# One DMA ring instead of two, with 64 KiB runs per partition, in a split-SiLU-multiply kernel

## The chip, the cores and the metric

The kernel runs on one core of a Trainium2 chip. The metric is device time in microseconds (us), the median of several runs. The core is fed by 16 DMA engines. A *ring* is the queue of transfers that one issuing engine owns: SP's ring is q1 in the profile and ACT's ring is q10. Both are worked off by the same 16 DMA engines.

## The reference

```python
batch, seq, dim = (32, 512, 2048)                # x: float32
half_dim = x.shape[-1] // 2
x1, x2 = x[..., :half_dim], x[..., half_dim:]
silu_x1 = x1 * (1 / (1 + np.exp(-x1)))
return (silu_x1 * x2).astype(np.float32)         # (32, 512, 1024)
```

That is 16384 rows of 8 KiB in and 4 KiB out: 134.2 MB to load and 67.1 MB to store, with one SiLU and one multiply per output element.

## The kernel before

The 128 rows per partition are cut into tiles of 4, then twenty times 6, then 4 rows. A load is 48 KiB per partition and a store 24 KiB. Loads are issued by SP and stores by ACT.

```python
K_MAIN, K_EDGE, KC = 6, 4, 2
in_pool  = ctx.enter_context(tc.tile_pool(name="in_pool", bufs=2))
out_pool = ctx.enter_context(tc.tile_pool(name="out_pool", bufs=4))
# ... plan = [(row0, K)]: 4, 6 x 20, 4 rows per partition ...
for bi, (row0, K) in enumerate(plan):
    xv = x_flat[row0:row0 + P * K].rearrange("(p k) d -> p k d", k=K)
    ov = out_flat[row0:row0 + P * K].rearrange("(p k) d -> p k d", k=K)
    xt = in_pool.tile([P, KT, in_cols], dt, name="xt")
    nc.sync.dma_start(out=xt[:, :K, :], in_=xv)                      # SP's ring
    ot = out_pool.tile([P, KT, half], dt, name="ot")
    for c in range(0, K, KC):
        ce = min(c + KC, K)
        nc.scalar.activation(out=ot[:, c:ce, :], in_=xt[:, c:ce, :half],
                             func=mybir.ActivationFunctionType.Silu)
        nc.vector.tensor_mul(out=ot[:, c:ce, :], in0=ot[:, c:ce, :],
                             in1=xt[:, c:ce, half:])
    nc.scalar.dma_start(out=ov, in_=ot[:, :K, :])                    # ACT's ring
```

## Time and profile before

| what | value | view |
|---|---|---|
| time | 474.58 us (474.44 to 474.65, 3 runs) | timed runs |
| span of the profiled run | 473.1 us | page, head |
| DMA engines' time in packets | 65.9% + 33.0% | page, part 3 |
| DVE, ACT busy | 30%, 25% | page, part 1 |

From the page of the kernel before: busy time per engine (part 1), DMA busy in tenths and GB/s in 40 slices of the span (part 2), the two rings with packets, MB and share of 16 engines (part 3), and the chain that ended last (part 4).

```profile
DVE 142.9 (30%) x64; ACT 118.9 (25%) x65; POOL 0.2 (0%) x4
...
DMA  8999999999999999999999999999999999999995
GB/s 355 449 398 424 432 430 455 420 428 451 414 432 441 432 443 432 416 434 447 426 428 457 418 435 436 443 432 424 432 443 418 438 453 411 451 432 418 433 420 244
...
q1 hardware_dynamic: 3168, 134.22, 65.9%
q10 hardware_dynamic: 3168, 67.11, 33.0%
...
DMA 78%; DVE 14%; ACT 4%; issue 1%; DVEq 0%; SPq 0%; ACTq 0%
```

The DMA engines are busy for nine tenths or more of every slice but the first and the last, and no compute engine is busy a third of the time. The kernel is bound by the DMA engines. What can be gained is the idle time at the ends and the time that packets take beyond their bytes. The last slice, at 244 GB/s, shows the end. The busy time by stretches of the kernel before, near its end (columns: stretch and its length; busy us of DVE, ACT and POOL; TensorE clock; DMA share; GB/s):

```profile
455.00:460.00 5.00, 0.00 (x0) 0.71 (x1) 0.00 (x0) 1.00 0.94 405
460.00:465.00 5.00, 3.77 (x2) 3.00 (x2) 0.00 (x0) 1.00 0.58 251
465.00:470.00 5.00, 0.72 (x1) 0.00 (x0) 0.00 (x0) 1.00 0.74 315
470.00:475.00 5.00, 0.00 (x0) 0.00 (x0) 0.00 (x0) 1.00 0.25 105
```

And its instructions in order of time (start us, duration, engine, line, operation):

```profile
459.29 3.71 ACT L64 ACTIVATE ot<-xt 128x2048 f32<-128x2048 f32 x2 [10.47 <-DMA xt<-in_x_dram]
461.23 4.49 DVE L69 TENSOR_TENSOR ot<-ot,xt 128x2048 f32<-128x2048 f32 x2 [9.29 <-ACT ot L64]
465.76 0.34 ACTq L74 DMA_DIRECT2D out_dram<-ot  x1
```

The last load lands at 459.3 us, but the last store is issued only at 465.8 us. In between the engines drain what is queued and then stand idle (share 0.58 between 460 and 465 us).

Part 3 of the page is made from records of single DMA packets: start, duration, size, ring. One packet here is the run of one partition. A record does not name its DMA engine, but engines can be told apart, since a packet starts within a few ns of the end of the one before it on the same engine. All that is said below of packets was worked out from these records in that way. In the kernel before, 48 KiB packets take 1815 ns, 24 KiB packets 912 ns, 32 KiB 1211 to 1213 ns and 16 KiB 611 ns. This is a straight line: 27.2 GB/s per engine plus about 8 ns per packet. I call the time on this line *nominal*, and what a packet takes beyond it *stretch*.

### The profile page before, as it was taken

The page shows a single profiled execution, that of the slowest core. Times are in us where ns is not written, and L with a number is a line of the kernel's source. Part 1 is how long each engine was busy: PE and PEld are TensorE (multiplying, and loading weights), DVE is VectorE, ACT ScalarE, POOL GpSimd, SP SyncE. Part 2 cuts the span into 40 slices and gives each one's busy share as a digit, 9 for nine tenths or more (in the row PEclk, how much of TensorE's full clock was granted, in tenths as well). Part 3 has the DMA queues.
Part 4 walks back from the last instruction along what each step waited for, and adds up shares of the span by engine and source line. Part 5 has one row for each costly group of instructions (what it writes and reads, how often), then busy time and mean ns, then how long its engine had stood idle before and what let it go on. Part 6 is the DMA issues. An engine that isn't in the chain of part 4 may idle for free.

```text
span 473.1 us, 296 instructions
## 1 busy us (share of the span) xinstructions
DVE 142.9 (30%) x64; ACT 118.9 (25%) x65; POOL 0.2 (0%) x4
## 2 busy tenths in 40 slices
DVE  0323505050514324050505142231505050513323
ACT  1340404041231404040413214040404042231411
POOL 0000000000000000000000000000000000000000
DMA  8999999999999999999999999999999999999995
GB/s 355 449 398 424 432 430 455 420 428 451 414 432 441 432 443 432 416 434 447 426 428 457 418 435 436 443 432 424 432 443 418 438 453 411 451 432 418 433 420 244
DMA packets 6338, 201.35 MB, mean 426 GB/s; under 512 B 704, under 2 KB 704, under 8 KB 704
## 3 DMA queue, kind: packets, MB, share of 16 engines
q1 hardware_dynamic: 3168, 134.22, 65.9%
q10 hardware_dynamic: 3168, 67.11, 33.0%
q14 instruction: 2, 0.02, 0.0%
HBM read 134.22 MB, written 67.11 MB: 426 GB/s over the span
## 4 chain that ended last, share of the span: by engine, by line
DMA 78%; DVE 14%; ACT 4%; issue 1%; DVEq 0%; SPq 0%; ACTq 0%
DMA xt<-in_x_dram 78%; DVE ot L69 14%; ACT ot L64 4%; DVEq L100 0%; SPq L59 0%; ACTq L64 0%
## 5 line engine op out<-in xcount | busy, mean ns | idle before, releaser
L69 DVE TENSOR_TENSOR ot<-ot,xt 128x2048 f32<-128x2048 f32 x64 | 142.9, 2287 | 322.8 <-ACT ot L64 322.8
L64 ACT ACTIVATE ot<-xt 128x2048 f32<-128x2048 f32 x64 | 117.6, 1899 | 343.4 <-DMA xt<-in_x_dram 343.4
L64 ACT ACT_TABLE_LOAD x1 | 1.3, 1283 | 0.7 <-PEq L89 0.7
L89 POOL MEMSET const-bfloat16-1.0<- 128x1 bf16 x1 | 0.1, 103 | 0.0
L89 POOL MEMSET const-uint8-127<- 128x1 uint8 x1 | 0.1, 103 | 0.0
L89 POOL MEMSET const-float32-1.0<- 128x1 f32 x1 | 0.1, 100 | 0.0
L89 POOL MEMSET const-float32-0.0<- 128x1 f32 x1 | 0.1, 99 | 0.2 <-issue 0.2
## 6 DMA issues: line engine op xcount, KB each, us to landing
xt<-in_x_dram SPq DMA_DIRECT2D x20, 6144.0 KB, 34.8
out_dram<-ot ACTq DMA_DIRECT2D x20, 3072.0 KB, 27.8
xt<-in_x_dram SPq DMA_DIRECT2D x2, 4096.0 KB, 20.7
out_dram<-ot ACTq DMA_DIRECT2D x2, 2048.0 KB, 15.4
```

The source lines that it names most:

```text
L64: nc.scalar.activation(out=ot[:, c:ce, :], in_=xt[:, c:ce, :half], func=mybir.ActivationFunctionType.Silu,)
L69: nc.vector.tensor_mul(out=ot[:, c:ce, :], in0=ot[:, c:ce, :], in1=xt[:, c:ce, half:],)
L89: nc = _bacc.Bacc("TRN2", target_bir_lowering=False, num_devices=1)
```

## The change

The intent: fewer, larger runs; one ring, so that every transfer has the engines to itself; and an end in which stores are queued ahead of the last multiply. Tiles become 8 rows, so a load is 64 KiB per partition. Two tiles share one output buffer, stored in one run of 64 KiB per partition. Everything is issued by SP in the order L0 L1 L2 S01 L3 L4 S23 L5 ... (L is a load, S a store of two tiles). The last two tiles are stored in a half and four quarters.

```diff
-    K_MAIN = 6
-    K_EDGE = 4
+    K = 8
-    out_pool = ctx.enter_context(tc.tile_pool(name="out_pool", bufs=4))
+    out_pool = ctx.enter_context(tc.tile_pool(name="out_pool", bufs=1))
+    xv = x_flat.rearrange("(n p h k) d -> n h p k d", p=P, h=2, k=K)
+    ov = out_flat.rearrange("(n p k) d -> n p k d", p=P, k=2 * K)
...
+    def load(i):
+        xt = in_pool.tile([P, K, in_cols], dt, name="xt")
+        nc.sync.dma_start(out=xt, in_=xv[i // 2, i % 2])
+        loaded[i] = xt
+    load(0)
+    load(1)
+    for i in range(n_tiles):
+        xt = loaded.pop(i)
+        if i % 2 == 0:
+            ot = out_pool.tile([P, 2 * K, half], dt, name="ot")
+        o0 = (i % 2) * K
         for c in range(0, K, KC):
+            o = slice(o0 + c, o0 + c + KC)
             ...                                  # SiLU and multiply as before, on ot[:, o, :]
+            if i == n_tiles - 1:
+                nc.sync.dma_start(out=ov[i // 2][:, o, :], in_=ot[:, o, :])
-        nc.scalar.dma_start(out=ov, in_=ot[:, :K, :])
+        if i == n_tiles - 2:
+            nc.sync.dma_start(out=ov[i // 2][:, :K, :], in_=ot[:, :K, :])
+        elif i % 2 == 1 and i < n_tiles - 2:
+            nc.sync.dma_start(out=ov[i // 2], in_=ot)
+        if i + 2 < n_tiles:
+            load(i + 2)
```

More of the change, by code (lines that the diff above doesn't have):

```diff
@@ L24 @@
     dt = x_flat.dtype
-    K_MAIN = 6
-    K_EDGE = 4
+    K = 8
     KC = 2
+    n_tiles = num_rows // (P * K)
+    assert n_tiles * P * K == num_rows
     in_pool = ctx.enter_context(tc.tile_pool(name="in_pool", bufs=2))
-    out_pool = ctx.enter_context(tc.tile_pool(name="out_pool", bufs=4))
-    rows_per_part_total = num_rows // P
-    rem = rows_per_part_total - 2 * K_EDGE
-    if rem > 0 and rem % K_MAIN == 0:
-        plan_k = [K_EDGE] + [K_MAIN] * (rem // K_MAIN) + [K_EDGE]
-    else:
-        plan_k = []
-        rem = rows_per_part_total
-        while rem > 0:
-            k = min(K_MAIN, rem)
-            plan_k.append(k)
-            rem -= k
-    plan = []
-    row = 0
-    for k in plan_k:
-        plan.append((row, k))
-        row += P * k
-    assert row == num_rows
-    KT = max(K_MAIN, K_EDGE)
-    for bi, (row0, K) in enumerate(plan):
-        xv = x_flat[row0:row0 + P * K].rearrange("(p k) d -> p k d", k=K)
-        ov = out_flat[row0:row0 + P * K].rearrange("(p k) d -> p k d", k=K)
-        xt = in_pool.tile([P, KT, in_cols], dt, name="xt")
-        nc.sync.dma_start(out=xt[:, :K, :], in_=xv)
-        ot = out_pool.tile([P, KT, half], dt, name="ot")
+    out_pool = ctx.enter_context(tc.tile_pool(name="out_pool", bufs=1))
+    xv = x_flat.rearrange("(n p h k) d -> n h p k d", p=P, h=2, k=K)
+    ov = out_flat.rearrange("(n p k) d -> n p k d", p=P, k=2 * K)
+    loaded = {}
+    def load(i):
[4 more added lines that the diff above has]
+    load(1)
+    ot = None
+    for i in range(n_tiles):
[3 more added lines that the diff above has]
+        o0 = (i % 2) * K
         for c in range(0, K, KC):
-            ce = min(c + KC, K)
+            o = slice(o0 + c, o0 + c + KC)
             nc.scalar.activation(
-                out=ot[:, c:ce, :],
-                in_=xt[:, c:ce, :half],
+                out=ot[:, o, :],
+                in_=xt[:, c:c + KC, :half],
                 func=mybir.ActivationFunctionType.Silu,
@@ L69 @@
             nc.vector.tensor_mul(
-                out=ot[:, c:ce, :],
-                in0=ot[:, c:ce, :],
-                in1=xt[:, c:ce, half:],
-            )
-        nc.scalar.dma_start(out=ov, in_=ot[:, :K, :])
+                out=ot[:, o, :],
+                in0=ot[:, o, :],
+                in1=xt[:, c:c + KC, half:],
+            )
+            if i == n_tiles - 1:
[6 more added lines that the diff above has]
+            load(i + 2)
 _INS = ['x']
```

## The prediction

> **What bounds the kernel now.** The 16 DMA engines. The page's part 1 shows DVE busy 30%, ACT 25%; part 2 DMA at 9 tenths in every slice but the first and last; part 3 65.9% + 33.0% of 16 engines' span; the chain of waits is 78% loads. The packet records behind part 3: a 48 KiB load packet takes 1815 ns, a 24 KiB store packet 912 ns, the edge tiles' 32 and 16 KiB ones 1211 and 611 ns. That is a line of 36.8 ns per 1000 bytes (27.2 GB/s per engine, 435 GB/s in all) plus about 8 ns per packet; the 435 agrees with the ceiling in the Trainium skill, "DMA: Bandwidth & Descriptors", Specifications. The rate is the same with loads alone (12 to 19 us), stores alone (the last 5 us) and both, and between two loads on one ring the gap is a few ns. So neither a second ring nor mixing costs anything visible.
>
> Sum for before: 1.7 us to the first packet + 466.7 us of packets per engine + 3.3 us idle per engine in the last 12 us + about 1.5 us closing = 473.1 us of span; timed, 1.5 us more.
>
> **What the change does.**
> - Packets: loads and full stores become 64 KiB (estimate from the line: 2419 ns). 224 packets per engine for 352, at 8 ns: -1 us; fewer semaphore packets: -0.1 us.
> - One ring, with SP waiting in order: L2, S01, L3, L4, S23, ... The output buffer is single, so a pair's first SiLU waits for the preceding store. With 1.9 + 4 x 2.29 = 11 us of compute per tile and an estimated 19.5 us per 8 MB transfer, the next load is issued about 13 us after that store lands, while another load still runs. The ring never runs dry; margin about 6 us. No gain, no loss.
> - Tail: when the last load lands, 4 MB of store (9.7 us) is queued, and four 1 MB stores follow from about 6 us on, 2.3 us apart, each lasting 2.4 us. So the idle 3.3 us at the end go: the main gain.
> - Head: unchanged; loads 0 and 1 are both queued.
> - A transient in before (36 load packets between 21 and 28 us took 2.0 to 2.6 us, about 1 us per engine) may or may not return.
>
> Sum for after: 1.7 + 464.9 + 0.6 (slow first packets) + 0.2 + 1.5 = 469 us of span, 470.4 us timed: 0.9% faster. All of it is on the critical path, since DMA is.
>
> Predicted 470.4 us, range 468.5 to 475. Faster by over 2%: 0.03 (it needs engines above 27.2 GB/s); within 2%: 0.89; slower by over 2%: 0.08.
>
> **What would show it.** 64 KiB packets at about 2419 ns, loads and stores alike; DMA at 9 tenths until the last slice; SiLU waiting for the store once per pair, without a hole in DMA; no idle in the last 12 us.
>
> **What would make it wrong.** (a) Address stride: a partition's loads now stand 128 KiB apart, so engines work at multiples of 512 KiB; the same page, "Latency and other measured facts", has copies losing rate at power-of-two pitches from 512 KiB up (207 of 214 GB/s). Packets above 2.42 us would show it; no run here does yet. (b) 64 KiB packets cut in two (+1 us). (c) A bubble where load and store switch on one ring, hidden before by the other ring. (d) The margin eaten by engines out of step: a hole per pair.

## The result, and the profile after

The changed kernel took 474.33 us (473.35 to 474.90, 4 runs) beside 474.55 us for the kernel before in the same rounds. The ratio is 0.9991, with a 95% interval of 0.9977 to 1.0006: no difference clear of noise. All outputs are right. I had predicted 470.4 us. The time lies inside my range, but the gain that I forecast, 4 us, is not there.

The same lines of the page of the changed kernel (parts 1 to 4):

```profile
DVE 142.4 (30%) x64; ACT 118.2 (25%) x65; POOL 0.2 (0%) x4
...
DMA  8999989999999999999999999999999999999996
GB/s 355 443 443 443 443 355 443 443 443 443 438 427 405 416 443 443 443 443 438 393 438 427 432 443 438 443 443 427 421 421 432 427 445 443 443 427 421 410 420 279
...
q1 hardware_dynamic: 4032, 201.33, 98.9%
...
DMA 79%; DVE 15%; ACT 3%; SPq 1%; DVEq 0%; issue 0%
```

The engines are as busy as before, now on one ring, and they moved the same bytes with 36% fewer packets. Yet the share of their time is still 98.9%. So the packets took longer than their bytes. Slice 5 (counted from 0, 59 to 71 us) drops to 355 GB/s. It is the slice in which the first store begins, and later slices dip to 405 and 393. A slice is a coarse measure, though, with packets of 2.4 us in slices of 11.8 us; the packet records are sharper.

Waits of the compute engines of the changed kernel (us in total, times, longest), then its stretches near the end, to be laid beside those of before:

```profile
ACT ot L58 <- DMA out_dram<-ot: 225.2, 7, 33.2
ACT ot L58 <- DMA xt<-in_x_dram: 115.7, 9, 20.5
```

```profile
455.00:460.00 5.00, 5.00 (x3) 4.81 (x3) 0.00 (x0) 1.00 0.87 374
460.00:465.00 5.00, 3.34 (x2) 0.00 (x0) 0.00 (x0) 1.00 1.01 428
465.00:470.00 5.00, 0.00 (x0) 0.00 (x0) 0.00 (x0) 1.00 0.77 324
470.00:475.00 5.00, 0.00 (x0) 0.00 (x0) 0.00 (x0) 1.00 0.02 8
```

The SiLU waits for the store seven times, once per pair after the first, as predicted, and this opens no hole in DMA. The hole between 460 and 465 us is filled (1.01 for 0.58). But look at the last row: in the last 3 us of the span the DMA share over 5 us is 0.02, and not 0. One engine is still at work. The packet records say it plainly: fifteen engines end between 468.1 and 469.6 us, and the sixteenth at 471.7 us, alone for its last seven packets.

The account, per engine, for both kernels and for a second profile of the changed one (run e0 below):

| term, us | predicted for after | before | after | after, second profile |
|---|---|---|---|---|
| packets at nominal time | 464.9 | 465.9 | 464.8 | 464.8 |
| stretch of each engine's first packet | 0.6 | 0.7 | 0.6 | 0.7 |
| stretch at the first store | left open, 0 in the sum | 1.1 | 1.2 | 1.1 |
| stretch later on | 0 | 0.1 | 1.4 | 1.6 |
| idle for want of transfers, at the end | 0 | 3.3 | 0 | 0 |
| last engine behind the mean of the 16 | 0.2 | 0.1 | 2.6 | 2.4 |

The rest of the span is the time to the first packet (1.7 us; 1.9 us in the mean of the engines), the closing (1.3 to 1.4 us), and overlaps of successive records (3 to 4 ns each; 1.4 us per engine before, 0.9 us after), which my sum left out. Nominal time came out as predicted: over 9 in 10 of the 64 KiB packets take 2415 to 2421 ns, loads and stores alike. The 3.3 us of idle at the end went, as predicted. They came back as 1.3 to 1.5 us more stretch and as one engine 2.4 to 2.6 us behind the mean. Both profiles of the changed kernel are of runs slower than the median (474.79 us for 474.33, 474.64 us for 474.43), and its runs scatter over 1.6 and 2.0 us, those of the kernel before in the same rounds over 0.2 and 0.9 us. So the stretch and the lag of a typical run may be somewhat smaller.

Where does the stretch stand? In the changed kernel, nearly all packets over 2480 ns are an engine's *last load packet before a store*: near 58, 117, 175, 233, 292, 350, 409 and 447 us. Those are the ends of L2, L4, L6 and so on, after which the ring holds a store. The change from store to load shows nothing, nor does the one from load to load. Over loads and stores that follow without such a change, the spread of the engines stays as it is, to 0.2 us. At each change from load to store the distance grows. Here is how far the last engine ends a transfer behind the first, at loads that stand just before a store in the changed kernel (two profiles), and at similar times in run e2, which has two rings:

```text
about us    22   61   119  177  235  293  351  410  448
after       0.5  0.6  0.8  1.3  1.7  2.1  2.7  3.2  3.5
after (e0)  0.8  0.8  0.9  1.3  2.0  2.4  2.8  3.1  3.5
e2          0.6  0.5  0.5  0.5  0.5  0.5  1.2  1.4  1.4
```

The kernel before, with two rings, behaves like e2: its first store leaves the engines 2.0 us apart, and at 433 us they are still 2.0 us apart. There the idle time at the end takes up the difference.

### The profile page after: what moved, and what is told of

Its sections match the earlier page's. It is cut to its first block, busy times and chain, and to the rows that moved or that the text cites. A ratio compares the mean times of both kernels' runs of the same rounds, so it can differ in the third digit from the quotient of the medians.

```text
span 473.0 us, 241 instructions
## 1 busy us (share of the span) xinstructions
DVE 142.4 (30%) x64; ACT 118.2 (25%) x65; POOL 0.2 (0%) x4
## 3 DMA queue, kind: packets, MB, share of 16 engines
q1 hardware_dynamic: 4032, 201.33, 98.9%
## 4 chain that ended last, share of the span: by engine, by line
DMA 79%; DVE 15%; ACT 3%; SPq 1%; DVEq 0%; issue 0%
DMA xt<-in_x_dram 79%; DVE ot L63 15%; ACT ot L58 3%; SPq L73 1%; DVEq L101 0%; SPq L45 0%
## 6 DMA issues: line engine op xcount, KB each, us to landing
out_dram<-ot SPq DMA_DIRECT2D x7, 28.3
```

## The experiments

Theory S: on one ring the change from load to store stretches the last load, and unevenly, so engines drift apart. Rival R: the slow packets are random hits of the memory and have nothing to do with the order. Rival G: the length of the store matters, not the number of changes. The first four kernels ran on one chip, five rounds each.

### e0: the changed kernel again

> The changed kernel unaltered, as the yardstick of this chip and for a second profile. Expected 474.3 us within 0.5. Theory S (switch): on one ring the last load packet before a store is stretched, so packets of over 2480 ns stand again only at the end of the loads that come just before a store (near 58, 117, 175, 233 ... us), about 2.5 us per engine in all, and one engine again ends 2 us or more after the rest. Rival R (the slow packets are random hits of the memory): the slow packets stand elsewhere than in the first profile.

Measured: 474.43 us (473.49 to 475.44) beside 474.56 us, ratio 0.9994 (0.9983 to 1.0005). The stretched packets stand at the same places: 58, 117, 175, 233, 291, 349, 408 and 446 us. One engine is again last, at 471.5 us, where the mean is 469.2 us. So R in its plain form, random places, falls.

### e1: each tile stored by itself, one ring

```diff
-        elif i % 2 == 1 and i < n_tiles - 2:
-            nc.sync.dma_start(out=ov[i // 2], in_=ot)
+        if i < n_tiles - 1:
+            nc.sync.dma_start(out=ov[i // 2][:, h0:h0 + K, :], in_=ot)
```
(with two output buffers of 8 rows in place of one of 16, and h0 = (i % 2) * K)

> One ring, the same 64 KiB loads, but each tile stored by itself in 32 KiB runs: 15 switches from load to store in place of 8. Theory S: 7 more stretched packets per engine at about 0.25 us: 1.7 us slower than the changed kernel, 476 us. Rival R (random hits), and rival G (the length of the store matters, not the number of switches): within 0.5 us of the changed kernel, 474.3 plus 0.5 us for 64 more packets per engine at 8 ns.

Measured: 476.31 us, ratio to before 1.0032 (1.0020 to 1.0044). That is 1.9 us over e0 with nearly twice the changes from load to store, 15 for 8. G, which expected 474.8 us, falls. The time is the one that S expected, but not by its sum: by the records stretch rose by 0.6 us and not by 1.7. The two profiled runs are 1.2 us apart (475.87 and 474.64 us); nominal time accounts for 0.5 us of that and stretch for the 0.6, while the last engine is 2.4 us behind the mean in both. The rest of the difference of the medians is not accounted for. Now six engines end at 471.7 to 472.6 us while the other ten end at 468.6 to 469.4 us.

### e2: the same tiles on two rings

```diff
-            nc.sync.dma_start(out=ov[i // 2][:, h0:h0 + K, :], in_=ot)
+            nc.scalar.dma_start(out=ov[i // 2][:, h0:h0 + K, :], in_=ot)
```

> As the run with one store per tile, but those stores are issued by ACT, so that they have their own ring and alternate with loads packet by packet. Theory S: the stretched load packets go except for those at the first store (about 1 us): 471 to 472 us, 4 to 5 us under the same tiles on one ring. Rival R, or a rival in which one slow engine alone sets the end: within 1 us of the same tiles on one ring.

Measured: 472.02 us (471.65 to 472.34), ratio to before 0.9945 (0.9933 to 0.9957), and 4.3 us under e1. The tiles, the packets and their sizes are e1's; only the ring of 15 stores differs. By the records each engine now takes loads and stores mostly in turn: between 60 and 440 us, 87% of its neighbouring packets are of different rings. The one ring of e1 and the two of e2, from their pages, then the last stretches of e2, to be laid beside those of the changed kernel:

```profile
q1 hardware_dynamic: 5040, 201.33, 99.0%
```

```profile
q1 hardware_dynamic: 2880, 138.41, 68.5%
q10 hardware_dynamic: 2160, 62.92, 31.0%
...
465.00:470.00 5.00, 0.00 (x0) 0.00 (x0) 0.00 (x0) 1.00 0.69 293
470.00:475.00 5.00, 0.00 (x0) 0.00 (x0) 0.00 (x0) 1.00 0.00 0
```

Between the first store, at 37 us, and the end of the loads only four packets are stretched by more than 60 ns, and all engines end within 0.7 us of each other, at 468.2 to 468.9 us. Stretch is down by 1.5 us, and the last engine is 0.3 us behind the mean in place of 2.4 us. The lagging engine is thus not one that is slow in itself. S holds here. One loss is left in e2: near 458 us, after the loads, 14 engines take 0.5 to 1.0 us too long for the first 8 KiB packet on SP's ring, which had been empty since 452 us (0.7 us per engine in all). Its cause was not tested.

### e3: the kernel before, all on one ring

```diff
-        nc.scalar.dma_start(out=ov, in_=ot[:, :K, :])
+        nc.sync.dma_start(out=ov, in_=ot[:, :K, :])
+        if bi + 2 < len(plan):
+            load(bi + 2)
```
(loads 0 and 1 are issued ahead of the loop)

> The kernel before with its 48 KiB loads and 24 KiB stores, but all on SP's ring, load i+2 issued behind store i: 21 switches from load to store. Theory S: 20 stretched packets at about 0.25 us cost 5 us, and the fuller queue at the end gains back up to 3 us: 476 to 478 us. Rival R: no stretch, only the gain at the end: 471 to 472 us.

Measured: 477.39 us, ratio 1.0047 (1.0034 to 1.0060). The time is as S expected, but half by luck. Later stretch was 2.4 us for the 20 changes after the first store, not 5, and the gain at the end did not come: the engines were idle 3.7 us there. Engines had drifted 4.9 us apart by then. A load has landed only when the last engine has brought its part, so the earliest engine waited 5.5 us for the last tile's store and the latest 0.5 us. Per change the stretch is 0.12 us here against 0.2 us in the changed kernel, whose stores are 2.7 times as long. But the mean hides that the stretch fades: 2.2 us of the 2.4 come in the first 14 changes, until about 335 us, and the last six, with the engines 4.9 us apart, add about 0.1 us. That hints that a change has no fixed price.

### e4 and e5: many more changes, on one ring and on two

In e4 every load is cut into four DMAs of 16 KiB per partition and every store into four of 8 KiB, and they alternate; e5 is the same with the stores on ACT's ring.

```diff
-        if i < n_tiles - 1:
-            nc.sync.dma_start(out=ov[i // 2][:, h0:h0 + K, :], in_=ot)
-        if i + 2 < n_tiles:
-            load(i + 2)
+        for c in range(0, K, KC):
+            if i < n_tiles - 1:
+                nc.sync.dma_start(out=ov[i // 2][:, h0 + c:h0 + c + KC, :], in_=ot[:, c:c + KC, :])
+            if nxt is not None:
+                piece(nxt, i + 2, c)       # a load of 2 rows per partition
```

> One ring, every load cut into four DMAs of 16 KiB per partition and every store into four of 8 KiB, in the order store, load, store, load: about 60 switches from load to store per engine in place of 15. Many more packets: about 472 us of packets per engine before any stretch (611 and 309 ns each). Theory S1 (each switch on a ring costs the engine a fixed time, 0.15 to 0.25 us): 9 to 15 us over the same pieces on two rings, 488 to 496 us. Theory S2 (the cost comes from long stretches in which all 16 engines read and then all write, and short pieces break them up): at most 2 us over the same pieces on two rings.

> The same pieces with the stores on ACT's ring, the control for the run with all of them on one ring. Both theories: the 472.02 us of the two-ring run with whole tiles plus the packets, about 7 us: 479 us, with stretched packets at the first store alone.

Measured: e4 476.51 us (476.35 to 476.95), e5 475.28 us (475.05 to 475.32), on one chip. Four times the changes cost 1.2 us over two rings, where e1 with a quarter of them cost 4.3 us over its own two-ring twin. So S1, a fixed price per change, falls: it wanted 9 to 15 us. The time of e5 was 475.28 us for my 479. The packets' nominal sum is 472.2 us as reckoned, but e5 has 1.1 us less stretch than e2, and with 1152 records per engine the overlaps of 3 to 4 ns, which I had left out, are 4 us.

### e8 and e4b: the same pieces in another order

This separates the order from the packet size. e8 has the very DMAs of e4 on the same ring, but four stores stand together and then four loads; e4b is e4 again beside it.

```diff
-        for c in range(0, K, KC):
-            if i < n_tiles - 1:
+        if i < n_tiles - 1:
+            for c in range(0, K, KC):
                 nc.sync.dma_start(out=ov[i // 2][:, h0 + c:h0 + c + KC, :], in_=ot[:, c:c + KC, :])
-            if nxt is not None:
+        if nxt is not None:
+            for c in range(0, K, KC):
                 piece(nxt, i + 2, c)
```

> One ring and exactly the pieces of the fine one-ring run, in another order: four store pieces together, then four load pieces together, so that load and store alternate in stretches of about 20 and 10 us again (15 switches in place of 60). Theory S1 (cost per switch) is already shaken: it expects this run faster. Theory S2 (long one-way stretches of all engines are what costs): 1.5 to 3 us slower than the fine order, 478 to 479.5 us, with stretched load packets at the end of load stretches and a slowest engine 2 us or more behind. Rival P (the stretch belongs to 32 to 64 KiB packets, not to the order): no slower than the fine order, 476.0 to 476.5 us.

> The fine one-ring run again, beside the grouped one: 476.5 us within 0.4, and few packets over 60 ns late after the first store.

Measured: e8 478.99 us (478.56 to 479.37), e4b 476.83 us (476.53 to 477.12). Grouping alone costs 2.2 us, with fewer changes of direction. Rival P (packet size) and what was left of S1 fall, and S2 holds: long one-way stretches on one ring are what costs. By the records of this one profile each, 0.4 us of it is stretch. Most is the last engine, which ends 2.9 us behind the mean in e8 and 1.2 us in e4b. The same ring, 99.5% full in e8 and 99.9% in e4b:

```profile
q1 hardware_dynamic: 18432, 201.33, 99.5%
```

```profile
q1 hardware_dynamic: 18432, 201.33, 99.9%
```

### e6: the end of the kernel before alone

```diff
+            if bi == len(plan) - 1:
+                nc.sync.dma_start(out=ov[:, c:ce, :], in_=ot[:, c:ce, :])
-        nc.scalar.dma_start(out=ov, in_=ot[:, :K, :])
+        if bi < len(plan) - 1:
+            nc.scalar.dma_start(out=ov, in_=ot[:, :K, :])
```

> The kernel before, its last tile alone stored in two 1 MB pieces from SP as each is multiplied. If the 3.3 us in which the engines stand idle at the end of the kernel before are on the critical path: about 1.9 us faster, 472.6 us, idle down to about 1.5 us. If they are not: 474.5 us.

Measured: 472.45 us (472.23 to 472.89), ratio 0.9954 (0.9942 to 0.9967). Idle at the end is 0.8 us for 3.3 us. In its stretches near the end the row of 460 to 465 us now reads 0.81 where before had 0.58:

```profile
460.00:465.00 5.00, 4.26 (x2) 2.50 (x2) 0.00 (x0) 1.00 0.81 346
465.00:470.00 5.00, 0.23 (x1) 0.00 (x0) 0.00 (x0) 1.00 0.76 315
```

So the part of my prediction about the end was sound: that idle time is on the critical path, and two small stores win 2 us without any other part of the change.

### e7: an early store

e2, with a memset tile stored to a scratch tensor at the start:

```diff
+    warm = out_pool.tile([P, 128], dt, name="warm", bufs=1)
+    scratch = nc.dram_tensor("scratch_dram", (P, 128), dt, kind="Internal").ap()
+    nc.gpsimd.memset(warm, 0.0)
+    nc.scalar.dma_start(out=scratch, in_=warm)
```

> The two-ring run with whole tiles, and a 64 KB store to a scratch tensor at the start, before any real store. If the 1 us of slow load packets that every kernel shows at its first store is a cost of the first write of a run, it moves under the wait for the first load: 471 us. If it belongs to the first large store: unchanged, 472.0 us.

Measured: 472.08 us, unchanged, and the stretch at the first large store (36 to 37 us) is still there, 1.1 us per engine. The early store's packets ran from 5 to 22 us, so it is no cost of the first write of a run. What it is stays open; e9 shows below that it is not tied to the first store either. The kernel before has it too, from 21 to 30 us, so it does not enter the comparison.

### e9: two rings, but the single output buffer kept

```diff
-            nc.sync.dma_start(out=ov[i // 2], in_=ot)
+            nc.scalar.dma_start(out=ov[i // 2], in_=ot)
```

> The changed kernel with its seven full stores moved back to ACT's ring, the tiles and the single output buffer kept. If a second ring alone were the cure: 470 to 472 us. My expectation: the store then shares the engines with two loads and lands some 12 us later, the next pair's first SiLU and so the next load wait for it, and the DMA engines stand idle for 1.5 to 5 us per pair: 480 to 500 us.

Measured: 511.44 us (509.97 to 512.79), ratio 1.0786 (1.0770 to 1.0803). The direction is mine, the size is not. From the DMA issues of e9 (count, median us from issue to landing), its waits, and a stretch in which it has two tiles to multiply and nothing to move:

```profile
out_dram<-ot ACTq DMA_DIRECT2D x7, 42.7
...
ACT ot L58 <- DMA out_dram<-ot: 326.9, 7, 48.8
...
100.00:110.00 10.00, 10.00 (x6) 10.00 (x6) 0.00 (x0) 1.00 0.31 105
```

The changed kernel's own seven full stores land 28.3 us after issue, since they do not share the engines:

```profile
out_dram<-ot SPq DMA_DIRECT2D x7, 28.3
```

With ACT's ring the store takes turns with the loads and lands 14 us later. In the first of these holes both next tiles have been loaded by then, both wait for the one buffer, and no further load may start until the first is multiplied. The engines are idle for 28 us each in all, and 9 us more of stretch than in the changed kernel stands in the records: at the first load packets after each hole, and at the last load packet before each store, which begins some 10 us later. I had reckoned a hole of 1.5 to 5 us per pair and no such stretch. At each of the seven stores this last load packet takes 0.9 to 1.1 us too long in the mean of the engines, as much as at the first store of the other kernels and more than at the changed kernel's later changes (0.04 to 0.4 us). So that loss is not tied to the first store of a run, and a second ring does not remove it by itself: in e9 ACT's ring runs empty before each store and loads run alone, in e2 loads and stores stay mixed. What decides between 1.1 us and the smaller loss stays open. The single ring is therefore not an error in itself: with one shared output buffer, its order is what lets the store pass quickly.

## Why the prediction was wrong

- **What bounds the kernel: right.** The DMA engines are full in both kernels.
- **Packet cost: right.** 2419 ns was estimated for 64 KiB and 2418 ns measured; the sum at nominal time is 464.8 us for 464.9.
- **The order on one ring leaves no hole: right.** The SiLU waits for the store seven times and DMA stays full.
- **The idle 3.3 us at the end go: right for fifteen engines.** e6 shows this gain by itself, 2 us of it. In the changed kernel the place of the idle is taken by one engine that is late. I had put 0.2 us for engines out of step; it is 2.4 to 2.6 us.
- **"So neither a second ring nor mixing costs anything visible": this step failed.** I had seen full rate with loads alone, with stores alone and with both, and one change from load to load. None of these is the change of all engines from a long run of loads to a long run of stores, which the kernel before never makes, since its two rings mix them. I listed that change as point (c) of what might be wrong, as a bubble, and gave the sum no term for it. What came is not a gap between packets but longer packets. The sum lacks 1.4 to 1.6 us of stretch and most of the 2.4 to 2.6 us of the late engine. Together they are about the 4 us of the gain; two more terms that it lacks, 1.2 us at the first store and 0.9 us of overlaps, nearly cancel. e1 against e2 shows that both belong to the one ring (4.3 us), and e4b against e8 that on one ring the order alone costs 2.2 us.
- **Point (a), the address stride, did not occur.** The Trainium skill, "DMA: Bandwidth & Descriptors", "Latency and other measured facts", lists losses, in copies between HBM tensors, for row pitches of 512 KiB and more; at the 128 KiB of this change over 9 in 10 packets run within 3 ns of 2418 ns. **Point (d)** was half right: engines do fall out of step, but what that costs is the end and not a hole per pair.

Why is the last load stretched, and why do engines drift apart rather than stay evenly late? The records give a pattern: at each of the seven changes after the first store in two profiles of the changed kernel, and at each of the first eleven in e1's, the eight engines that came later to the change had a longer mean stretch than the eight that came earlier (for instance 417 against 333 ns near 233 us, and 353 against 182 ns near 350 us). That fits an engine that still loads while others already store being slowed by them, so that the late become later. But the same records speak against this as the whole cause. Near 233 us the engine that comes first to the change is itself stretched by 251 ns, though no engine begins a store packet before it does. And at the changes of e1 near 390 and 449 us six engines started their last load packet 3 to 4 us after the first engine, ran most of it while the others stored, and took no more than 8 ns too long. So why the last load is stretched, and why the engines drift, stays open; shown is that both come with long one-way stretches on one ring.

The version that beats both kernels is e2: 64 KiB loads on SP's ring, a 32 KiB store per tile on ACT's ring, two output buffers, and the end of the changed kernel. It is 0.55% under the kernel before.

## What to carry to other kernels

When DMA is the bound, count three things apart: bytes at the packet rate, stretch, and how late the last engine is. A ring that alternates long runs of loads with long runs of stores can lose a few us to the last two even though nearly every slice of the page says 9 tenths. Two rings that mix loads and stores left the last engine 0.3 us behind the mean (e2), fine alternation on one ring 1.2 to 1.3 us (e4, e4b), the long stretches 2.4 to 2.9 us (changed kernel, e1, e8); but the fine pieces cost 7 us of nominal time. And look first at what the engines do after the last load: two small stores there (e6) won 2.0 us, and the best rebuilding (e2) 2.5 us.

## What the Trainium skill lacked or had wrong

- "DMA: Bandwidth & Descriptors", "Issuing engines are not separate DMA queues", says that issuing from several engines only saves the sequencer's time of starting a DMA. Here moving 15 stores from SP to ACT saved 4.3 us of 476.3 us (e1 to e2). The SP issues take 0.34 us each and were not the bound: the ring decides the order in which the 16 engines meet loads and stores.
- The same page has no word on a change of direction on one ring. Here the last load packet before a store takes up to 0.9 us more than its 2418 ns after the first store, and the spread of the engines grew from 0.5 to 3.5 us over the run; transfers that follow without such a change added at most 0.2 us.
- No page has the stretch at the first large store: 0.8 to 1.2 us per engine in the kernels with whole tiles, not removed by a small early store (e7), and 0.9 to 1.1 us again at each of the seven stores of e9.
- In "Latency and other measured facts" of that page the list of row pitches starts at 512 KiB; a pitch of 128 KiB, with runs of 64 KiB, showed no loss here (2418 ns per packet, 27.1 GB/s per engine).
- Where the page is borne out: its Specifications give a ceiling of 435 GB/s for the 16 engines, and the line through packets has 16 times 27.2 GB/s, the same number.
